# Start of a two-layer hybrid encoder: halves of x in two transfers each, squares on two engines, pair sums, constant products in the first norm, a weight split ahead of its root

## The chip, the cores and the metric

The kernel runs on one core of a Trainium2 chip. The metric is the device time of one execution in microseconds; less is better. TensorE (PE) multiplies, VectorE (DVE) and ScalarE (ACT) work elementwise, GpSimd (POOL) helps, SyncE (SP) issues most of the loads. All data are float32.

## What is computed

Two encoder layers over 512 positions of 1024 channels. The part that matters here is the start of the first layer: the norm of x, the product with the input projection `w_in`, and, for the memory branch, the norm of the memory tokens.

```python
def rms_norm(x, g):
    xf = x.astype(jnp.float32)
    y = xf * lax.rsqrt(jnp.mean(xf * xf, axis=-1, keepdims=True) + RMS_EPS)
    return (y * g.astype(jnp.float32)).astype(x.dtype)

mem_n = rms_norm(mem, mem_norm_g)
for l in range(DEPTH):
    h = rms_norm(x, g_pre_mix[l])
    proj = h @ w_in[l]
    q_a, k_a, v_a, q_b, k_b, v_b, q_m, gate_pre = jnp.split(proj, splits, axis=-1)
    ...                       # three attention branches (the third into mem_n), gates, output projection
    x = x + rms_norm(merged @ w_out[l], g_post_mix[l])
    ...                       # gated MLP with a depthwise convolution
    x = x + rms_norm(f @ w_down[l], g_post_ffn[l])
```

## The kernel before

x lies transposed, channels on the partitions: eight blocks of 128 channels (k = 0 to 7) by 512 positions, in two halves of 256 positions (`HALVES`). Every product is made three times: a weight and an activation are each split into a high part (a cast to the faster matmul type, on ScalarE) and a low part (the difference to it, on VectorE or GpSimd), and `mm3` adds high by high, high by low and low by high. `split` does the cast and the difference; `weights` loads a weight of 128 x 1024 (three buffers `wraw`) and splits it, for the first group in two pieces of 512 columns each (tiles `m`).

The start of the program, in the order of its code: `load_x` issues the first half of x from SyncE in four transfers of two blocks; two constant products (`idle`) run on TensorE; `first_squares` squares the eight blocks on ScalarE and adds neighbours in pairs on VectorE; `pre_norm_job` makes the norm. Its `rstd_job` sums over the channels by products with a constant column (`mean`; these are the sums spoken of later), takes the root on ScalarE and the reciprocal on VectorE, and spreads the result over the partitions by two transposes on TensorE. Then, for each k, VectorE multiplies x with the gain and this row (`normed`), ScalarE casts it to the high part of h, VectorE makes the low part.

The first six output tiles of `w_in` (`FIRST`) are made by `run_group`, in three pairs, first for the first half of the positions and then for the second: 8 blocks x 2 tiles x 3 products = 48 products for each pair and half. For the second half the squares stand behind the first half's last cast of h; their sums are two times two products.

What the order is decided by: each engine runs its instructions in the order of the program. `Woven` holds jobs (generators) with a due time on a clock that counts TensorE's planned cost; `tick` and `need` run the jobs whose time has come and so place their instructions in the order. The second half's `pre_norm_job` is spawned with a delay of `SD1`, the norm of the memory tokens (`mem_norm_job`: four loads issued by ScalarE, eight squares, seven adds, the sums) with 6.0. `Counted` books the planned time of ScalarE and VectorE for the due times of other jobs. A scheduler below orders instructions of one engine by their dependences and the order of the code. `wraw` has three buffers, so the load of the fourth weight waits for the differences of the first.

Of the kernel before, what the change touches and what calls it, by code (L numbers as in the profile page):

```python
# [9 lines left out]
AF = mybir.ActivationFunctionType  # L10
# [10 lines left out]
KD = D_MODEL // 128  # L21
# [4 lines left out]
HALVES = (slice(0, 256), slice(256, 512))  # L26
FULL = slice(0, 512)
FIRST = (0, 3, 4, 7, 6, 1)
# [3 lines left out]
V_PRE, V_POST, V_PREF, V_POSTF, V_BG, V_CW, V_CB = 0, 8, 16, 24, 32, 56, 188  # L32
# [3 lines left out]
LAT_QK, LAT_SM, LAT_T, LAT_V, LAT_T2 = 1.0, 4.5, 1.5, 2.0, 0.6  # L36
STEP_A, STEP_B, STEP_M = 9.0, 9.0, 5.5
SQG, LOG, GEN, KVE = {0: (), 1: ()}, {0: (), 1: ()}, 'GGVGVG', 'VVGG'
SD1 = 4.0
MARGIN = 0.3  # L40
SB = True
TAILG = (0, 2, 4, 6)
# [77 lines left out]
def tile_hybrid_encoder(ctx, tc, xT, memT, memg, vecs, rpb, w_in, w_kv, w_bra, w_brb, w_brm,  # L120
                        w_out, w_up, w_down, c_ident, c_mask, c_tab0, c_tab1, out):
    nc = tc.nc
# [14 lines left out]
    wv = Woven(tc)  # L137

    def nm(s):
        uid[0] += 1  # L140
        return f"{s}_{uid[0]}"
# [11 lines left out]
    def ytile(shape=(128, 512)):  # L153
        return tp.tile(list(shape), F32, tag="y", name=nm("y"), bufs=8)
# [4 lines left out]
    def smalls(n=2):  # L159
        return sp.tile([128, n], F32, tag="st", name=nm("st"))  # L160
# [7 lines left out]
    def tbank(shape=(128, 512)):  # L168
        return ps_t.tile(list(shape), F32, tag="pt", name=nm("pt"))

    def obank(p=64):
        return ps_o.tile([p, 512], F32, tag="o", name=nm("o"))
# [5 lines left out]
    ACT, V = Counted(nc.scalar, wv, 0.1, 0.8e-3), Counted(nc.vector, wv, 0.065, 1.05e-3)  # L178
# [8 lines left out]
    xs = const.tile([128, 2, KD, 256], F32, name="x")  # L187

    def xh(k, half):
        return xs[:, half.start // 256, k, :]  # L190

    def load_x(half):
        for k in range(0, KD, 2):
            i = half.start // 256
            nc.sync.dma_start(out=xs[:, i, k:k + 2, :], in_=xT[:, i, k:k + 2, :])

    g0 = const.tile([128, KD], F32, name="g0")
    nc.scalar.dma_start(out=g0, in_=vecs[:, 0, V_PRE:V_PRE + KD])
    load_x(HALVES[0])
    eps = const.tile([128, 1], F32, name="eps")  # L200
    nc.gpsimd.memset(eps, RMS_EPS)
# [25 lines left out]
    def weights(src, K, C, slot=None, eng=None, after=None):  # L227

        raw = wp.tile([128, K, C], F32, tag="wraw", name=nm("wraw"))
        nc.sync.dma_start(out=raw, in_=src)  # L230
        if slot is None:
            hi = wp.tile([128, K, C], F32R, tag="whi", name=nm("whi"), bufs=2)
            lo = wp.tile([128, K, C], F32R, tag="wlo", name=nm("wlo"), bufs=2)
            split(raw, hi, lo, eng)
            behind(last_copy[0], after)
            return [(hi[:, k, :], lo[:, k, :]) for k in range(K)]
        n = 512 // C
        w = []
        for k in range(0, K, n):
            c = min(n, K - k)  # L240
            hi, lo = slot(F32R, (128, c, C)), slot(F32R, (128, c, C))
            split(raw[:, k:k + c, :], hi, lo, eng)
            w += [(hi[:, i, :], lo[:, i, :]) for i in range(c)]
        return w

    def mm(ps, a, b, first, last, cost):
        wv.pe(nc.tensor.matmul(ps, a, b, start=first, stop=last), cost)  # L247
# [75 lines left out]
    def acctile():  # L323
        return small("acc", 2, (128, 512))

    def rstd_job(accs, n, box):

        nb = n // 128
        bank = tbank((128, n + nb))
        pr, pt = bank[:, 0:n], bank[:, n:n + nb]  # L330
        for i, a in enumerate(accs):
            for b in range(nb):
                mm(pt[:, b:b + 1], a[:, 128 * b:128 * b + 128], mean, i == 0 and b == 0,
                   i == len(accs) - 1 and b == nb - 1, 0.11)
        rs = smalls(nb)
        crit[0] = ACT.activation(rs, pt, AF.Sqrt, bias=eps, scale=1.0).ins
        V.reciprocal(rs, rs)
        yield 0.8
        for b in range(nb):
            one = rs[:, b:b + 1]  # L340
            spread = bass.AP(one.tensor, one.offset, [list(one.ap[0]), [0, 128]])
            wv.pe(nc.tensor.transpose(pr[:, 128 * b:128 * b + 128], spread, ident), 0.11)
        box.append(pr)

    def normed(src, g, rs, hi, lo, eng=None):
        h32 = small("h32", 3)
        V.scalar_tensor_tensor(out=h32, in0=src, scalar=g, in1=rs, op0=ALU.mult, op1=ALU.mult)
        split(h32, hi, lo, eng)
# [7 lines left out]
    def rtile():  # L356
        return tp.tile([128, 512], F32, tag="R", name=nm("R"), bufs=1)
# [3 lines left out]
        V.tensor_mul(y, ps, R)  # L361
        return y

    def pre_norm_job(l, goff, acc, hs, i):
        half, box = HALVES[i], []
        yield from rstd_job(acc if isinstance(acc, list) else [acc[:, half]], 256, box)
        for k in range(KD):
            g = g0[:, k:k + 1] if l == 0 and goff == V_PRE else vec[:, l, goff + k:goff + k + 1]
            normed(xh(k, half), g, box[0], hs[k][0][:, half], hs[k][1][:, half],
                   G if k in LOG[l > 0 and goff == V_PRE] else V)  # L370
        crit[0] = last_copy[0]
        yield 1.2
        wv.give(f"h{l}.{goff}.{i}")
# [5 lines left out]
    def end_job(l, goff, og, acc, acc2, i, then, lat, more=()):  # L379
        half, box = HALVES[i], []  # L380
        yield lat
        yield from rstd_job([acc[:, half]] + list(more), 256, box)
        for k in range(KD):
            V.tensor_mul(og[k][:, half], og[k][:, half], box[0])
            (G if then is None and i and k in TAILG else V).tensor_add(xh(k, half), xh(k, half), og[k][:, half])
            if acc2 is not None:
                sumsq_add(acc2[:, half], xh(k, half), k == 0, None, G if k in SQG[goff == V_POSTF] else V)
            else:
                nc.sync.dma_start(out=out[:, k, half], in_=xh(k, half))
        if then is not None:  # L390
            yield 9.0
            yield from then(i)

    def factor_end_job(l, goff, og, acc, acc2, i, nxt):

        half, box = HALVES[i], []
        gnext, h, R = nxt
        yield ready(1.4)
        yield from rstd_job([acc[:, half]], 256, box)
        for k in range(KD):  # L400
            V.tensor_mul(og[k][:, half], og[k][:, half], box[0])
            V.tensor_add(xh(k, half), xh(k, half), og[k][:, half])
            raw_split(l, gnext, k, xh(k, half), h[k][0][:, half], h[k][1][:, half])
            if k == 0:
                yield 0.6
            wv.give(f"h{l}.{gnext}.{i}.{k}")
            yield 1.05
        for k in range(KD):
            sumsq_add(acc2[:, half], xh(k, half), k == 0)
        yield 3.5  # L410
        box = []
        yield from rstd_job([acc2[:, half]], 256, box)
        ACT.copy(R[:, half], box[0])
        if i == 1:
            yield 0.6
            wv.give(f"R{l}.{gnext}")
# [30 lines left out]
    def h_tiles():  # L447
        return [(htile(), htile()) for _ in range(KD)]
# [46 lines left out]
    def group_weights(srcs, engs):  # L495
        return [weights(s, KD, 128, big, e) for s, e in zip(srcs, engs)]
# [368 lines left out]
    def first_squares(half):  # L865
        sqs = [ytile((128, 256)) for _ in range(KD)]
        for k in range(KD):
            ACT.activation(sqs[k], xh(k, half), AF.Square)
            if k % 2:
                V.tensor_add(sqs[k], sqs[k], sqs[k - 1])  # L870
            if k in (3, 5) and half != HALVES[0]:
                V.tensor_add(sqs[k], sqs[k], sqs[k - 2])
        return sqs[1::2] if half == HALVES[0] else sqs[5::2]

    idle_bank = obank(128)

    def idle(n):

        one, none = mean[:, 0:1], zero[:, 0:1]
        a, b = (bass.AP(t.tensor, t.offset, [list(t.ap[0]), [0, w]]) for t, w in ((one, 128), (none, 512)))  # L880
        for _ in range(n):
            mm(idle_bank, a, b, True, True, 0.0)

    idle(2)
    hs = h_tiles()
    wv.spawn(pre_norm_job(0, V_PRE, first_squares(HALVES[0]), hs, 0))
    gw = group_weights([w_in[0, m] for m in FIRST[:2]], (V, V))
    load_x(HALVES[1])
    nc.sync.dma_start(out=vec, in_=vecs)
    nc.gpsimd.tensor_scalar_mul(hb, vec[:, :, V_BG:V_CW], 0.5)  # L890
    wv.need(f"h0.{V_PRE}.0")
    with tc.issue_after(last_copy[0]):
        sqs = first_squares(HALVES[1])
    wv.spawn(pre_norm_job(0, V_PRE, sqs, hs, 1), SD1)
    gw += group_weights([w_in[0, m] for m in FIRST[2:]], (V, G, V, G))
# [6 lines left out]
    for l in range(depth):  # L902
# [29 lines left out]
        acc = [None] * KD  # L932
# [20 lines left out]
        hs, R, gw = h_tiles(), rtile(), []  # L953
# [17 lines left out]
        for j in range(NFF):  # L971
            pair = []
            for m in (j, j + NFF):
# [3 lines left out]
                w = ahead.pop()  # L977
# [24 lines left out]
        else:  # L1002
            hm, km, vm = [], [], []
            wv.spawn(mem_norm_job(l + 1, hm, htile), 20.0)
            pre, R, raw, box = [], rtile(), [], []
# [5 lines left out]
            gw = []  # L1011
# [19 lines left out]
            hs = box  # L1031
# [93 lines left out]
```

## Time and profile before

| | |
|---|---|
| median of 3 runs | 1551.7 us (1549.61, 1551.70 and 2167.76) |
| profiled execution, its own time | 1551.73 us |
| its span | 1550.0 us |
| TensorE busy | 1522.5 us, 98% |
| VectorE busy | 951.6 us, 61% |
| ScalarE busy | 712.7 us, 46% |
| GpSimd busy | 149.7 us, 10% |
| share of TensorE in the chain that ended last | 91% |

The chain is followed back from the last instruction, at each step to what released it. Times in the rows are microseconds from the start of the span. A product of float32 columns that isn't in the faster type shows as two records, so two sums show as x4.

### The profile page before, as it was taken

The page shows a single profiled execution, that of the slowest core. Times are in us where ns is not written, and L with a number is a line of the kernel's source. Part 1 is how long each engine was busy: PE and PEld are TensorE (multiplying, and loading weights), DVE is VectorE, ACT ScalarE, POOL GpSimd, SP SyncE. Part 2 cuts the span into 40 slices and gives each one's busy share as a digit, 9 for nine tenths or more (in the row PEclk, how much of TensorE's full clock was granted, in tenths as well). Part 3 has the DMA queues.
Part 4 walks back from the last instruction along what each step waited for, and adds up shares of the span by engine and source line. Part 5 has one row for each costly group of instructions (what it writes and reads, how often), then busy time and mean ns, then how long its engine had stood idle before and what let it go on. Part 6 is the DMA issues. An engine that isn't in the chain of part 4 may idle for free.

```text
span 1550.0 us, 20648 instructions
## 1 busy us (share of the span) xinstructions
PE 1522.5 (98%) x7970; PEld 1300.1 (84%) x7970; DVE 951.6 (61%) x1684; ACT 712.7 (46%) x1266; POOL 149.7 (10%) x217
## 2 busy tenths in 40 slices
PE   8999999999999999999989999999999999999997
PEld 7988888888988888888888888888889888888887
DVE  6685676335777777742497756753456977776233
ACT  5565554336544444532355555532354544444231
POOL 3340000110000000000154300002100000000000
PEclk9999999999999999999999999999999999999999
DMA  7221213235113322333431221132350233323331
GB/s 246 89 88 64 62 57 107 84 95 165 53 59 100 100 96 95 118 90 101 129 102 59 78 66 58 61 104 88 102 177 15 82 96 99 101 99 89 99 105 63
DMA packets 45810, 144.91 MB, mean 93 GB/s; under 512 B 5376, under 2 KB 9600, under 8 KB 45712
## 3 DMA queue, kind: packets, MB, share of 16 engines
q1 hardware_dynamic: 43776, 139.85, 28.5%
q10 hardware_dynamic: 1296, 2.10, 0.4%
q0 software_dynamic: 640, 1.64, 0.3%
q8 instruction: 62, 1.02, 0.3%
q14 instruction: 36, 0.29, 0.1%
HBM read 141.48 MB, written 2.10 MB: 93 GB/s over the span
## 4 chain that ended last, share of the span: by engine, by line
PE 91%; DVE 6%; ACT 2%; issue 1%; DMA 0%; SPq 0%; ACTq 0%; DVEq 0%
PE mm L247 80%; PE s L247 4%; PE o L247 3%; PE pt L258 2%; DVE m L114 1%; DVE y L114 1%; PE pt L247 1%; DVE ka L114 1%; DVE x L114 1%; ACT y L114 1%; DVE st L114 0%; DVE acc L114 0%; DMA x<-in_xT_dram 0%; DVE wlo L114 0%; ACT whi L114 0%
## 5 line engine op out<-in xcount | busy, mean ns | idle before, releaser
L247 PE MATMUL mm<-h,whi 128*128 128x512 f32 x2496 | 776.5, 392 | 0.0
L247 PEld LDWEIGHTS mm<-h,whi 128*128 128x128 f32 x2496 | 462.0, 188 | 91.3
L247 PE MATMUL mm<-h,wlo 128*128 128x512 f32 x1248 | 486.9, 390 | 0.0
L114 DVE TENSOR_TENSOR wlo<-wraw,whi 128x1024 fp32r<-128x1024 f32 (+1 forms) x213 | 259.2, 1217 | 284.7 <-ACT whi L114 282.3
L114 ACT CAST whi<-wraw 128x1024 fp32r<-128x1024 f32 (+1 forms) x213 | 221.4, 1040 | 307.8 <-PE mm L247 293.4
L247 PEld LDWEIGHTS mm<-h,wlo 128*128 128x128 f32 x1248 | 234.5, 188 | 49.6
L247 PE MATMUL mm<-m,whi 128*128 128x512 f32 (+1 forms) x800 | 215.1, 356 | 1.0 <-DVE m L114 0.8
L247 PEld LDWEIGHTS mm<-m,whi 128*128 128x128 f32 x800 | 141.8, 189 | 22.8 <-PE mm L247 1.3
L247 PE MATMUL mm<-m,wlo 128*128 128x512 f32 (+1 forms) x400 | 142.1, 355 | 0.0
L114 DVE SCALAR_TENSOR_TENSOR y<-y,vec,y 128x511 f32<-128x511 f32 x176 | 130.5, 748 | 3.5 <-ACT y L114 0.9
L114 DVE TENSOR_TENSOR y<-mm,R 128x512 f32<-128x512 f32 x82 | 56.4, 688 | 68.5 <-PE mm L247 68.5
L247 PEld LDWEIGHTS mm<-m,wlo 128*128 128x128 f32 x400 | 75.5, 189 | 10.9
L802 POOL TENSOR_TENSOR m<-m,y 128x512 f32<-128x512 f32 x28 | 36.1, 1289 | 399.4 <-DVE y L114 399.4
L114 ACT ACTIVATE y<-y,vec 128x512 f32<-128x512 f32 x88 | 71.1, 815 | 2.3 <-DVE y L114 1.9
L247 PE MATMUL mm<-m,m 128*128 128x512 f32 x240 | 63.5, 394 | 0.0
L114 ACT ACTIVATE y<-y 128x512 f32<-128x512 f32 x44 | 27.9, 633 | 71.7 <-DVE y L114 71.3
L114 ACT CAST m<-pt 128x512 fp32r<-128x512 f32 (+1 forms) x72 | 38.6, 541 | 46.8 <-PE pt L258 38.5
L114 ACT ACTIVATE y<-y,st 128x256 f32<-128x256 f32 (+1 forms) x80 | 43.8, 549 | 30.4 <-DVE st L114 28.9
L114 DVE TENSOR_TENSOR acc<-acc,sq 128x256 f32<-128x256 f32 (+1 forms) x80 | 41.1, 514 | 26.6 <-ACT sq L114 24.7
L114 DVE TENSOR_TENSOR m<-pt,m 128x512 fp32r<-128x512 f32 (+1 forms) x72 | 45.1, 630 | 19.9 <-ACT m L114 18.6
L114 ACT CAST m<-y 128x512 fp32r<-128x512 f32 x32 | 19.9, 622 | 72.5 <-DVE y L114 72.5
L247 PE MATMUL mm<-h,m 128*128 128x256 f32 x312 | 49.1, 301 | 2.0 <-ACT h L114 1.0
(154 smaller groups left out, 1789.9 us busy)
## 6 DMA issues: line engine op xcount, KB each, us to landing
wraw<-in_w_in_dram SPq DMA_DIRECT2D x88, 512.0 KB, 3.7
wraw<-in_w_up_dram SPq DMA_DIRECT2D x88, 512.0 KB, 3.6
wraw<-in_w_down_dram SPq DMA_DIRECT2D x32, 512.0 KB, 3.5
wraw<-in_w_out_dram SPq DMA_DIRECT2D x16, 512.0 KB, 3.9
wraw<-in_w_down_dram SPq DMA_DIRECT2D x16, 384.0 KB, 3.1
wraw<-in_w_kv_dram SPq DMA_DIRECT2D x8, 512.0 KB, 4.0
wraw<-in_w_bra_dram SPq DMA_DIRECT2D x16, 192.0 KB, 2.3
x<-in_xT_dram SPq DMA_DIRECT2D x8, 256.0 KB, 7.3
```

What stands on the lines that cost most here:

```text
L114: return op(*args, **kw)
L247: wv.pe(nc.tensor.matmul(ps, a, b, start=first, stop=last), cost)
L258: wv.pe(nc.tensor.transpose(ps[:, 128 * i:128 * i + 128], s, ident), 0.11)
L802: (V if br == 2 and m >= 6 else G).tensor_add(acc[m], acc[m], gs)
```

## The change

`load_x` brings each half of x in two transfers of four blocks. In the first half, `first_squares` squares blocks 3 and 7 on VectorE instead of ScalarE; the pair sums stay. `rstd_job` can be given `idle` as `warm` and then puts constant products of 256 columns between its own: one after the second pair sum, one after the reciprocal, two after the transposes; only the first norm does so. The first weight's split is written ahead of the first norm's job, the second behind it. `SD1` is 5.0 instead of 4.0.

```diff
-SD1 = 4.0
+SD1 = 5.0
...
     def load_x(half):
-        for k in range(0, KD, 2):
+        for k in range(0, KD, 4):
             i = half.start // 256
-            nc.sync.dma_start(out=xs[:, i, k:k + 2, :], in_=xT[:, i, k:k + 2, :])
+            nc.sync.dma_start(out=xs[:, i, k:k + 4, :], in_=xT[:, i, k:k + 4, :])
...
-    def rstd_job(accs, n, box):
+    def rstd_job(accs, n, box, warm=None):
...
+            if warm and i == 1:
+                warm(1, 256)
         rs = smalls(nb)
         crit[0] = ACT.activation(rs, pt, AF.Sqrt, bias=eps, scale=1.0).ins
         V.reciprocal(rs, rs)
+        if warm:
+            warm(1, 256)
         yield 0.8
...
+        if warm:
+            warm(2, 256)
         box.append(pr)
...
         for k in range(KD):
-            ACT.activation(sqs[k], xh(k, half), AF.Square)
+            if half == HALVES[0] and k in (3, 7):
+                V.tensor_mul(sqs[k], xh(k, half), xh(k, half))
+            else:
+                ACT.activation(sqs[k], xh(k, half), AF.Square)
...
-    def idle(n):
+    def idle(n, w=512):
...
-            mm(idle_bank, a, b, True, True, 0.0)
+            mm(idle_bank[:, 0:w], a, b, True, True, 0.0)
...
-    wv.spawn(pre_norm_job(0, V_PRE, first_squares(HALVES[0]), hs, 0))
-    gw = group_weights([w_in[0, m] for m in FIRST[:2]], (V, V))
+    sqs = first_squares(HALVES[0])
+    gw = group_weights([w_in[0, FIRST[0]]], (V,))
+    wv.spawn(pre_norm_job(0, V_PRE, sqs, hs, 0, idle))
+    gw += group_weights([w_in[0, FIRST[1]]], (V,))
```

What this does to the order is seen at three places. The first is ScalarE around the root of the first half's norm (`st` from `pt`); `y` are the squares, `wraw_148` and `wraw_158` the first and the second weight, `m` their high parts, `h_112` and `h_114` the first high parts of h. Before:

```order
L114 ACTIVATE y_134<-x 128x256
L114 ACTIVATE y_135<-x 128x256
L114 ACTIVATE st_183<-pt_174,eps 128x2
L114 CAST m_150<-wraw_148 128x512
L114 CAST m_154<-wraw_148 128x512
L114 CAST h_112<-h_39_188 128x256
L114 CAST m_160<-wraw_158 128x512
L114 CAST h_114<-h_40_192 128x256
```

Of the change (the first weight is now `wraw_146`, the second `wraw_156`):

```order
L114 ACTIVATE y_131<-x 128x256
L114 ACTIVATE y_132<-x 128x256
L114 CAST m_148<-wraw_146 128x512
L114 ACTIVATE st_180<-pt_170,eps 128x2
L114 CAST m_152<-wraw_146 128x512
L114 CAST m_158<-wraw_156 128x512
L114 CAST m_162<-wraw_156 128x512
L114 CAST h_110<-h_39_188 128x256
```

The cast of half the first weight has moved ahead of the root, and all four casts of the two weights now stand ahead of the first cast of h.

The second place is TensorE at the end of the first pair of tiles (`mm_285` and `mm_286`) for the first half, where the sums of the second half's squares stand (`pt` from `mean` and `y`). Before:

```order
L247 MATMUL mm_286<-h_124,m_165 128x256
L247 MATMUL pt_333<-mean,y_225 128x1 x2
L247 MATMUL pt_333<-mean,y_227 128x1 x2
L247 MATMUL mm_285<-h_126,m_154 128x256
L247 MATMUL mm_285<-h_127,m_154 128x256
```

Of the change:

```order
L247 MATMUL mm_286<-h_124,m_163 128x256
L247 MATMUL pt_339<-mean,y_225 128x1 x2
L247 MATMUL pt_339<-mean,y_227 128x1 x2
L247 MATMUL o_287<-h_110,m_244 128x256
L247 MATMUL o_287<-h_111,m_244 128x256
```

Before, `h_124` is block 6 of h and the six products of block 7 (`h_126`, `h_127`) follow the sums; in the change `h_124` is block 7, so all 48 products of the pair stand ahead of the sums and the next pair's follow.

The third place is ScalarE after that, at the second half's norm. `h_112`, `h_114` and so on are again the high parts of h, now of the second half; `m_387` to `m_393` are the memory tokens, `h_95_395` and `sq` their squares, `wraw_272` the sixth weight of the group. Before:

```order
L114 CAST h_112<-h_83_355 128x256
L114 CAST h_114<-h_84_359 128x256
L114 CAST m_274<-wraw_272 128x512
L114 CAST m_278<-wraw_272 128x512
L114 CAST h_116<-h_85_363 128x256
L455 DMA m_387<-in_memT_dram 128x512
L114 CAST h_118<-h_86_367 128x256
L114 CAST h_120<-h_87_371 128x256
L455 DMA m_389<-in_memT_dram 128x512
```

Of the change, from the last of the four loads on (`m_359`; `whi` are the first two weights of the memory branch):

```order
L461 DMA m_359<-in_memT_dram 128x512
L114 ACTIVATE h_87_361<-m_353 128x256
L114 ACTIVATE sq_88_363<-m_353 128x256
...
L114 ACTIVATE sq_93_378<-m_359 128x256
L114 CAST h_110<-h_95_392 128x256
L114 ACTIVATE sq_94_381<-m_359 128x256
L114 CAST h_112<-h_96_396 128x256
L114 CAST whi_702<-wraw_700 128x1024
L114 CAST whi_743<-wraw_741 128x1024
L114 CAST h_114<-h_97_400 128x256
```

The casts of the second half's h have moved behind the memory loads and seven of the eight squares of the memory tokens, and from the third on behind two whole weight casts too; VectorE's differences and adds stand in the same new order.

## Rows read from the trace of the kernel before

**Rows 1.** The page: busy time of each engine, chain by engine.

```profile
PE 1522.5 (98%) x7970; PEld 1300.1 (84%) x7970; DVE 951.6 (61%) x1684; ACT 712.7 (46%) x1266; POOL 149.7 (10%) x217
PE 91%; DVE 6%; ACT 2%; issue 1%; DMA 0%; SPq 0%; ACTq 0%; DVEq 0%
```

**Rows 2.** The chain in order of time, 0 to 100 us: start, length, what.

```profile
2.12 6.74 DMA x<-in_xT_dram
...
23.54 1.05 PE pt L247 x8
...
37.15 5.04 PE mm L247 x42
42.19 0.34 PE pt L247 x4
```

**Rows 3.** Transfers by issue window: the first weight; the first load of x's second half.

```profile
wraw<-in_w_in_dram SPq DMA_DIRECT2D x1, 512.0 KB, 7.5
...
x<-in_xT_dram SPq DMA_DIRECT2D x1, 256.0 KB, 8.6
```

**Rows 4.** Timeline, 0 to 30 us: start, length, engine, line, what, idle before.

```profile
0.74 1.81 SPq L195 DMA_DIRECT2D x<-in_xT_dram  x4
...
2.60 0.91 SPq L230 DMA_DIRECT2D wraw<-in_w_in_dram  x2
...
5.88 0.72 ACT L114 ACTIVATE y<-x 128x256 f32<-128x256 f32 x2 [0.47 <-DMA x<-in_xT_dram]
...
11.17 0.26 ACT L114 ACTIVATE st<-pt,eps 128x2 f32<-128x2 f32 x1 [1.56 <-PE pt L247]
...
11.68 0.69 PE L342 MATMUL pt<-ident,st 128*128 128x128 f32 x2 [0.56 <-DVE st L114]
12.41 0.48 DVE L114 SCALAR_TENSOR_TENSOR h<-x,g,pt 128x256 f32<-128x256 f32 x1 [0.78 <-PE pt L342]
...
14.87 7.81 PE L247 MATMUL mm<-h,m 128*128 128x256 f32 x41 [0.91 <-DVE h L114]
...
20.44 2.57 ACT L114 ACTIVATE y<-x 128x256 f32<-128x256 f32 x8
...
21.28 2.54 DVE L114 TENSOR_TENSOR y<-y,y 128x256 f32<-128x256 f32 x6
```

**Rows 5.** Constant products; then busy time of tile mm by stretch, granted clock.

```profile
0.95 3.78 PE L247 MATMUL o<-zero,mean 128*128 128x512 f32 x4 [0.95 <-POOL zero L206]
...
14.87:17.62 2.75, 2.75 (x12) 2.69 (x12) 0.00 (x0) 0.00 (x0) 1.00 0.64 206
...
20.00:22.68 2.68, 2.68 (x22) 2.48 (x20) 0.00 (x0) 0.00 (x0) 1.00 0.88 337
```

**Rows 6.** VectorE's groups, 12 to 24 us: count, busy us, mean ns, idle before.

```profile
L114 DVE TENSOR_TENSOR m<-wraw,m 128x512 fp32r<-128x512 f32 x6 | 4.1, 689 | 0.0
L114 DVE SCALAR_TENSOR_TENSOR h<-x,g,pt 128x256 f32<-128x256 f32 x8 | 3.6, 471 | 0.8 <-PE pt L342 0.8
L114 DVE TENSOR_TENSOR h<-h,h 128x256 fp32r<-128x256 f32 x8 | 3.2, 414 | 0.0
```

**Rows 7.** Timeline, 29 to 42 us, of the second half's norm and the memory tokens.

```profile
29.57 0.33 ACTq L455 DMA_DIRECT2D m<-in_memT_dram  x1
...
32.85 0.80 ACT L114 CAST h<-h 128x256 fp32r<-128x256 f32 x2 [1.25 <-DVE h L114]
33.13 1.08 DVE L114 TENSOR_TENSOR h<-h,h 128x256 fp32r<-128x256 f32 x3
...
41.38 2.35 DVE L114 TENSOR_TENSOR wlo<-wraw,whi 128x1024 fp32r<-128x1024 f32 x2
```

**Rows 8.** Transfers by issue window: memory loads (one, three), one late weight.

```profile
m<-in_memT_dram ACTq DMA_DIRECT2D x1, 256.0 KB, 5.2
m<-in_memT_dram ACTq DMA_DIRECT2D x3, 256.0 KB, 5.9
...
wraw<-in_w_in_dram SPq DMA_DIRECT2D x1, 512.0 KB, 3.6
```

More of the change, by code (lines that the diff above doesn't have):

```diff
@@ L362, in scaled, with pre_norm_job @@
         return y
-    def pre_norm_job(l, goff, acc, hs, i):
+    def pre_norm_job(l, goff, acc, hs, i, warm=None):
         half, box = HALVES[i], []
-        yield from rstd_job(acc if isinstance(acc, list) else [acc[:, half]], 256, box)
+        yield from rstd_job(acc if isinstance(acc, list) else [acc[:, half]], 256, box, warm)
         for k in range(KD):
@@ L875, in tile_hybrid_encoder @@
     idle_bank = obank(128)
-    def idle(n):
+    def idle(n, w=512):
         one, none = mean[:, 0:1], zero[:, 0:1]
-        a, b = (bass.AP(t.tensor, t.offset, [list(t.ap[0]), [0, w]]) for t, w in ((one, 128), (none, 512)))
+        a, b = (bass.AP(t.tensor, t.offset, [list(t.ap[0]), [0, w]]) for t, w in ((one, 128), (none, w)))
         for _ in range(n):
-            mm(idle_bank, a, b, True, True, 0.0)
+            mm(idle_bank[:, 0:w], a, b, True, True, 0.0)
     idle(2)
     hs = h_tiles()
-    wv.spawn(pre_norm_job(0, V_PRE, first_squares(HALVES[0]), hs, 0))
-    gw = group_weights([w_in[0, m] for m in FIRST[:2]], (V, V))
+    sqs = first_squares(HALVES[0])
+    gw = group_weights([w_in[0, FIRST[0]]], (V,))
+    wv.spawn(pre_norm_job(0, V_PRE, sqs, hs, 0, idle))
+    gw += group_weights([w_in[0, FIRST[1]]], (V,))
     load_x(HALVES[1])
```

## Prediction

> **What bounds the kernel now.** I read the page's busy shares and chain first, then the chain in order of time, then the timeline of the first 45 us, and last the landings of single transfers. TensorE is busy for 1522.5 us, 98% of the span, and carries 91% of the chain that ended last [rows 1]. So the reader is to see that little is left outside TensorE, and that the change, whose code all lies ahead of the first 45 us, can at most move the point from which TensorE runs without a break. The chain shows that point. It runs through the fourth transfer of x until 8.86, through squares, sums and the first norm, and meets TensorE for good at 23.54, where the sums of the second half's squares begin [rows 2]. From there TensorE never waits until 42.19, when 42 of the 48 products of the second half's first pair of output tiles are done [rows 2]. After that the order of every engine is the same as before, so I compare the two kernels at that event: each microsecond there is one in the end. The sum is made against the profiled execution's 1551.73 us; the median of the three runs is 1551.70, so no correction is needed.
>
> **First half, up to its root.** Today the last 256 KB of the first half of x land 6.7 us after their issue at 2.12 [rows 2], though the third transfer had landed by 5.88 [rows 4]. Now the same last bytes are in the second of two transfers. Its issue comes at about 1.18 instead of 2.12, since four issues took 1.81 us, 0.47 each [rows 4], and two go. The bounds are 5.88 (the landing of the third piece) and 8.86 (that of the fourth). The nearest row is the fourth's own 6.74 us, as the bytes and their place behind the others are the same, so I take 1.18 + 6.74 = 7.92.
>
> From landing t, the old chain needs two squares, an add, two sums, root (at 11.17), reciprocal and two transposes (to 12.37): t + 2.3 at the root, t + 3.5 at the end [rows 4]. Now three squares stand on ScalarE (k = 4, 5, 6; one more at 0.32, which is 2.57 / 8) while VectorE squares k = 7 beside them; so t + 2.6 = 10.5 at the root and t + 3.8 = 11.7 at the end. The square moved to VectorE thus saves one of four, but four pieces arrive at once where two did. The constant product after the reciprocal is half as wide as one of the two that took 3.78 us [rows 5], so 0.95 us at that pace; it can hold the transposes by 0.2 us, which VectorE hides: it is still in the second weight difference until 11.9. The two later constant products end at 13.8, before the first low part of h (14.4, below). Without those covers they would cost up to 0.2 and 1.9 us.
>
> **The weight split ahead of the root.** ScalarE now casts half of the first weight before the root, so the root waits for that weight if it is late. The first weight took 7.5 us from 2.60 [rows 3, 4]; issued 0.94 earlier it lands at 9.2, the cast's 0.52 of issue room ends at 9.7, and the root is due at 10.5. So it holds nothing, with 0.8 us to spare. VectorE does the difference in its idle time. But on ScalarE three more weight casts now stand ahead of the first cast of h, so the first low part of h comes at 14.4; today TensorE has it at 14.87 [rows 4]. (The chain: root 10.5, casts 0.52 apart, the last of the three ends at 12.3, the cast of h behind it at 12.8; VectorE from 11.9 on has two norm products, two weight differences and this low part, 2.7 us by their means [rows 6], 2.4 with the overlap shown below.)
>
> **From there to the sums of the second half.** VectorE worked from 12.41 to 21.37 without idle time on 8 products with the norm, 8 low parts and 5 weight differences, 9.0 us for 10.2 us of busy time (3.6, 3.2 and five sixths of 4.1 [rows 6]), as they overlap. After the root it still has 8, 8 and 5 (the first has gone ahead, but the difference m_249 has come in), of which one (m_153) runs in the 0.7 us of the transposes. So it starts its norm products at 11.9, needs 8.3 us and ends at 20.2, 1.2 us earlier. ScalarE is free for the second half's squares some 1.2 us before that, at 19.0, and finishes them by 21.6. The six adds (2.54 us [rows 4]) then end at 22.7 on VectorE, which now is the later of the two; today they end at 23.82. TensorE's four sums end 0.77 later, at 23.5 against 24.59 [rows 2]. With SD1 at 5.0 all 48 products of the first pair stand before these sums, where 42 did. The 6 that no longer follow are 0.72 us at 0.12 each [rows 2]. Today 102 products and two transposes lie between 24.59 and the second half's first product at 37.15 [rows 2], 12.56 us; now 6 products fewer, so the second half can begin at 23.5 + 11.84 = 35.3. This part gains 1.8 us.
>
> **What the moved spawn does to the second half.** The larger SD1 also puts the memory norm's start ahead of the second half's norm. ScalarE then has, in this order: four loads of the memory tokens, seven squares of them, and only then the first cast of h for the second half; two whole weight casts stand before the third. Today those casts ended at 33.65, 3.5 us before TensorE wanted the first of them, and the memory squares came after [rows 7]. The new chain: sums at 23.5; root, then casts at 0.52 each, so the last weight cast starts at 25.3; four issues of 0.33 behind it, the last at 26.3. Its landing is bounded by 5.2 us (the first such load) and 8.6 (the longest of an x transfer, in the crowd at the start); I take 5.9, the median of the other three [rows 3, 8], so 32.2. The seventh square and the cast follow, and VectorE starts the first low part at 33.0. Up to its last low part it then has 8 low parts of 0.36, 3 adds and 6 norm products of 0.42, and 2 whole weight differences of 1.18 [rows 4, 7]: 2.9 + 1.3 + 2.5 + 2.4 = 9.0 us. The last low part ends at 42.0 and the seventh of eight at 41.6; after the seventh the five products that need it or follow it take 0.6 us, so the 42 products are done at 42.2. Unhindered they would be done at 35.3 + 5.04 = 40.3, so TensorE waits 1.9 us in pieces, mostly before the low parts k = 2 and k = 4, each behind a weight difference. Who waits behind these waits: ScalarE's casts of the two kv weights, whose products stand behind all pairs of the second half, so nobody.
>
> **The sum.** At the event of 42.19 the new kernel stands at 42.2: 1.8 us gained by a first half that ends earlier and hands 6 products less to the time behind its sums, and 1.9 us given back because h of the second half comes late. That is +0.0 against 1551.73, so **1551.7 us**. The other edits cost nothing: the first constant product lies where TensorE waits for the second transfer anyway (from about 6 to 8 us), and the two issues saved in the second half of x hand over data that is not squared before 19.0.
>
> **The rivals.** First, *x lands early*: the second transfer comes at 5.88, as its bytes arrive in one run. Everything up to the event moves by 2.04, to 1549.7. For it: the third piece was there 4.2 us after its issue at about 1.65 [rows 4]. Against it: the fourth took 6.74.
> Second, *the second half does not wait*: the memory loads land within 4.0 us, as a lone weight did in 3.6 [rows 8], and the casts of h are in time: 1551.7 - 1.9 = 1549.8. Against it: the four share the DMA engines with two kv weights.
> Third, *slower: the memory loads crowd*. They land 8.6 us after issue, as the first load of the second half of x did [rows 3]. The price is 8.6 - 5.9 = 2.7 us, so 1554.4; from a landing of 5.9 us on the event comes later than today. For it: four loads and two weights, 2 MB, now leave within a few microseconds, where today the four were spread from 29.57 on, one after another behind casts [rows 7]. Beside it stands a sentence of the Trainium skill, "DMA: Bandwidth & Descriptors", section "Issuing engines are not separate DMA queues": loads issued by ScalarE interleave with those of SyncE on the same DMA engines, so a queue of their own does not shield them. No run here shows yet by how much.
> Fourth, *TensorE's pace*. In 14.87 to 17.62 it issued 12 products in 2.75 us, from 20.00 on 22 in 2.68; the granted clock reads 1.00, the 2.4 GHz level, in both [rows 5], so the count tells more here than the column. If the first pair kept the slow 0.23 us to its end, its 48 would end at 14.4 + 11.0 = 25.4 and hold the sums by 2.7 us: 1554.4. If the pace rises at 20 as today, they end at 22.9 and cost 0.2; if the constant products raise it earlier, nothing is gained, as the sums wait for 22.7 anyway. The Trainium skill's "TensorE: Matmul & The Clock Gate", section "Part 1: The HAM clock gate", says that an idle array runs at half clock and that sustained work releases it; by that rule short constant products with pauses between them buy little, and the trace agrees in so far as the two wide ones at the start left the pace slow at 14.87.
> Fifth, *x lands as late as it did*: 8.86, since larger transfers need not end sooner. Then 0.94 of the gain is missing: 1552.6.
>
> **How the numbers follow.** Forecast 0.38, early x 0.20, no wait 0.17, crowded loads 0.10, slow pace 0.05, late x 0.10. By its own costs the forecast goes from 1551.0 (memory loads at 5.2) to 1552.6 (x at 8.86). The range takes in both cases just below 1550 and, beside an early x, loads at 5.2 (another 0.7 lower) and 0.4 of the 2.1 us between the two close runs shown: 1548.6. Above, it takes in the crowded loads and the slow pace: 1554.5. A change of 2%, about what a measurement of this kernel can tell from no change, would be 31 us, and no case comes near: faster 0.01, same 0.98, slower 0.01.
>
> **What would show it.** Right: the four sums of the second half start near 22.7; the last load of memory tokens lands near 32; TensorE's first products of the second half start near 35.3 and show gaps behind low parts of h. Wrong: the second transfer of x well off 7.9; the root waiting for the first weight; no gaps between 35 and 42; or the event of 42.19 moved by more than 1 us, which would make the second half's delay, the step that I hold for the least sure, the wrong one.

## The result, and the profile after

The changed kernel takes 1555.26 us (median of 22 runs, 1550.34 to 1560.37), the kernel before 1551.36 in the same comparison. The ratio is 1.0026, with a 95% interval of 1.0019 to 1.0034: 3.9 us slower. 1551.7 was predicted, with a range up to 1554.5. The runs of the change lie 10 us apart; those of before, one at 2167.76 left aside, 4.7; in the later comparisons those of before lie 4.8 to 8.8 us apart.

I have two profiles of the changed kernel: one of an execution with a span of 1551.2 us, and one taken later (below) with 1553.8, which lies nearer to the median. The page of the first, its busy shares and its chain, against [rows 1]:

```profile
PE 1525.0 (98%) x7978; PEld 1302.2 (84%) x7978; DVE 952.8 (61%) x1686; ACT 710.2 (46%) x1264; POOL 150.5 (10%) x217
PE 91%; DVE 6%; issue 1%; ACT 1%; DMA 1%; POOL 0%; ACTq 0%; DVEq 0%; POOLq 0%
```

Little here tells the two kernels apart. TensorE is busy for 2.5 us more, and the four new constant products, eight records, alone took 0.68 + 1.20 + 1.74 = 3.6. The chain in order of time (start, length, what) shows the difference, against [rows 2]:

```profile
6.70 0.54 PE o L247 x2
...
8.30 1.06 PE o L247 x2
...
19.64 1.84 DVE y L114 x2
21.53 1.02 PE pt L247 x4
...
24.53 6.84 DMA m<-in_memT_dram
...
43.80 0.34 PE pt L247 x4
```

In [rows 2] the chain comes to TensorE at 23.54 and stays there. Now it leaves TensorE again for the last load of the memory tokens and the second half's h, and TensorE takes it over only at the end of the first pair. The event by which I compared the kernels, 42 products of that pair done, is at 43.80 instead of 42.19. The timeline (start, length, engine, line, what, idle before), against [rows 4, 7]:

```profile
5.68 1.03 ACT L114 ACTIVATE y<-x 128x256 f32<-128x256 f32 x3 [0.25 <-DMA x<-in_xT_dram]
...
7.35 0.62 ACT L114 CAST m<-wraw 128x512 fp32r<-128x512 f32 x1 [0.64 <-DMA wraw<-in_w_in_dram]
...
8.34 0.26 ACT L114 ACTIVATE st<-pt,eps 128x2 f32<-128x2 f32 x1 [0.37 <-PE pt L247]
...
20.12 0.61 PE L247 MATMUL pt<-mean,y 128*128 128x1 f32 x4 [1.06 <-DVE y L114]
21.53 1.01 PE L247 MATMUL pt<-mean,y 128*128 128x1 f32 x4 [0.80 <-DVE y L114]
...
30.95 5.92 PE L247 MATMUL s<-h,m 128*128 128x256 f32 x48
36.71 3.16 PE L247 MATMUL mm<-h,m 128*128 128x256 f32 x25
...
40.77 3.02 PE L247 MATMUL mm<-h,m 128*128 128x256 f32 x17 [0.90 <-DVE h L114]
```

x came early: the second transfer was there at 5.7. The first weight at 7.3 did not hold the root, which waited for TensorE. The second half then starts at 36.9 and stops for h. (The timeline lets a product start up to 0.16 us before the one ahead of it ends; I count from that end, 30.95 + 5.92 = 36.87, as the chain in [rows 2] does.) Its 42 products take 43.80 - 36.87 = 6.9 us instead of 5.04 [rows 2]. The granted clock is the other new thing. Columns: stretch, its length, PE busy (instructions), granted clock, DMA share, GB/s.

```profile
20.00:22.00 2.00, 1.08 (x7) 0.81 0.54 207
22.00:24.00 2.00, 2.00 (x10) 0.50 0.32 50
...
26.00:28.00 2.00, 2.00 (x11) 0.50 0.98 293
28.00:30.00 2.00, 2.00 (x19) 0.98 1.02 366
```

Each of TensorE's two groups of sums stands behind a pause, of 1.06 and 0.80 us, and the clock fell to the 1.2 GHz level for some 6 us: 10 and 11 products in 2 us, 19 at the 2.4 GHz level. From the end of the sums at 22.55 to 36.87 lie 14.3 us for what takes 11.84 at full pace, so 2.5 us were lost there.

### The profile page after: what moved, and what is told of

It is laid out like the page before. It is cut to its first block, busy times and chain, and to the rows that moved or that the text cites. A ratio compares the mean times of both kernels' runs of the same rounds, so it can differ in the third digit from the quotient of the medians.

```text
span 1551.2 us, 20650 instructions
## 1 busy us (share of the span) xinstructions
PE 1525.0 (98%) x7978; PEld 1302.2 (84%) x7978; DVE 952.8 (61%) x1686; ACT 710.2 (46%) x1264; POOL 150.5 (10%) x217
## 4 chain that ended last, share of the span: by engine, by line
PE 91%; DVE 6%; issue 1%; ACT 1%; DMA 1%; POOL 0%; ACTq 0%; DVEq 0%; POOLq 0%
PE mm L247 80%; PE s L247 4%; PE o L247 3%; PE pt L258 2%; DVE y L114 1%; DVE m L114 1%; PE pt L247 1%; DVE h L114 1%; DVE ka L114 1%; DVE x L114 1%; DVE acc L114 1%; DVE wlo L114 0%; DMA m<-in_memT_dram 0%; ACT whi L114 0%; ACT y L114 0%
## 5 line engine op out<-in xcount | busy, mean ns | idle before, releaser
L114 DVE TENSOR_TENSOR m<-wraw,m 128x512 fp32r<-128x512 f32 (+1 forms) x58 | 37.9, 668 | 24.0 <-ACT m L114 23.8
```

Source lines behind the costliest of these rows:

```text
L114: return op(*args, **kw)
```

## Experiments

Two theories stood against each other first. **A**: the second half's h is late, because SD1 at 5.0 puts it behind the memory tokens on ScalarE and VectorE. **B**: the clock that falls around the second half's sums costs the time. All comparisons are with runs of the kernel before on the same chip.

**SD1 alone, on the kernel before.**

```diff
-SD1 = 4.0
+SD1 = 5.0
```

> The kernel before with SD1 5.0 and nothing else. Theory A: the second half's casts of h come behind the memory squares as in the change; by the chain of the prediction the sums end at 24.6, the last load of the memory tokens lands 8.7 later, the 42 products are done 18.7 after the sums: 43.3 against 42.19, so about 1552.5, and the spread of the runs widens as the change's did. Rival C: SD1 alone is harmless or gains the 0.7 us of six products: 1550.7 to 1551.4, spread as before.

Measured: 1557.35 us, ratio 1.0043 (1.0030 to 1.0057), 6.7 us slower. The chain of this kernel:

```profile
27.12 9.23 DMA m<-in_memT_dram
...
42.52 2.96 DMA wraw<-in_w_kv_dram
45.47 0.94 DVE h L114
...
48.94 0.34 PE pt L247 x4
```

The last of the four loads takes 9.2 us here, where I had 5.9. The chain then names a load of a kv weight, which would have held VectorE until 45.5. The timeline does not bear that out: VectorE worked without a pause from 38.47 to 47.5, and ScalarE had cast both kv weights of that stretch before 41.

```profile
38.47 0.76 DVE L114 TENSOR_TENSOR h<-h,h 128x256 fp32r<-128x256 f32 x1 [0.79 <-ACT h L114]
...
41.45 4.67 POOL L599 TENSOR_TENSOR y<-mask,y 128x256 f32<-128x256 f32 x3 [2.00 <-DVE h L114]
...
43.86 1.68 DVE L114 TENSOR_TENSOR wlo<-wraw,whi 128x1024 fp32r<-128x1024 f32 x1
45.46 1.28 DVE L114 TENSOR_TENSOR h<-h,h 128x256 fp32r<-128x256 f32 x2
```

The event, expected at 43.3, is at 48.94. The last load landed 3 us later than expected, the first low part stands 2.1 us behind it instead of 0.8, and VectorE's chain of low parts took 10.0 us instead of 9.0, slow beside GpSimd. The one number is enough to make the kernel slower than the whole change does.

**SD1 undone, in the change.**

```diff
-SD1 = 5.0
+SD1 = 4.0
```

> The change with SD1 back at 4.0, all else kept: the sums of the second half stand again behind 42 products, and the memory norm behind the second half's norm. Theory A (the longer time comes from the second half's norm, which SD1 at 5.0 puts behind the memory loads and squares): the loss goes, 1551 to 1552, near the kernel before, and between 33 and 43 us TensorE shows no gap behind h. Rival (one of the other parts costs the time: large transfers, the constant products, the squares on VectorE, or the first weight's cast ahead of the root): it stays at 1554 to 1556. If the other parts are a gain of their own, as my sum had it (0.7 to 2 us), 1549.5 to 1551.

Measured: 1551.45 us, ratio 1.0001 (0.9990 to 1.0012). The whole loss is SD1's, and at this SD1 the other parts together are worth nothing that can be measured. In its profile TensorE runs through the pair:

```profile
35.17 5.04 PE mm L247 x42
```

This execution, the fastest of the ten, has a span of 1545.6 and its event at 40.21, 2.0 us ahead of [rows 2]; its clock did not fall behind the sums. (Its span is 4.4 us shorter; the rest is far behind the event, see the last section.) The runs of this kernel go from 1547.5 to 1553.8, so what the other parts gain is had in some of them at most.

**The memory norm later, SD1 left at 5.0.**

```diff
-    wv.spawn(mem_norm_job(0, hm, big), 6.0)
+    wv.spawn(mem_norm_job(0, hm, big), 8.0)
```

> The change with the memory norm spawned at 8.0 instead of 6.0: the 48 products stay ahead of the sums, but the second half's casts of h stand ahead of the memory squares again. Theory A (the late second-half norm costs): the wait of TensorE at 37 to 44 us (7.09 us for 42 products that need 5.04 in the change's trace) goes, 42 products done near 41.8 instead of 43.80, so 2.0 us below the change, near 1553.2, and the spread of the runs narrows. Theory B (only the clock that fell to 0.50 from 21.6 to 28.0 costs): the norm in time gains nothing that lasts, time stays near 1555. Rival C (the larger transfers of x scatter the time): near 1555, spread as wide as the change's 10 us.

Measured: 1551.48 us, ratio 1.0001 (0.9992 to 1.0011). Its chain passes the second half's first pair without a break:

```profile
37.23 5.76 PE mm L247 x48
```

So A holds: what costs is not that 48 products stand ahead of the sums, but that the memory norm stands ahead of the second half's.

**Constant products around the second half's sums.**

```diff
+            if keep:
+                idle(keep[i], 256, keep_bank)
...
-    wv.spawn(pre_norm_job(0, V_PRE, sqs, hs, 1), SD1)
+    wv.spawn(pre_norm_job(0, V_PRE, sqs, hs, 1, None, (2, 2)), SD1)
```

Two of 256 columns stand ahead of each of the two sums, in a bank of their own.

> The change with constant products of 256 columns in a bank of their own, two ahead of each of the two sums of the second half, so that TensorE does not idle from 18.9 to 21.5. The granted clock should then read 1.00 where the change had 0.50 (21.6 to 28.0), and the second half's products can begin near 34.2 instead of 36.7. Theory A: the event of 43.80 is set by memory loads, squares and casts and stays within 0.5 us, so time near 1555. Theory B: the 2.5 us that the slow products cost come off, 1552.8.

Measured: 1558.12 us, ratio 1.0040 (1.0026 to 1.0055). The clock stays at 1.00 from 20 to 36 us, and it is not faster:

```profile
26.15 8.35 DMA m<-in_memT_dram
...
44.45 4.00 PE mm L247 x17
```

TensorE reaches the second half earlier, and waits longer for an h that isn't there; then the clock falls in these pauses, and 17 products take 4.00 us instead of 2.04. The event did not stay within 0.5 us of 43.80, as A expected; it is at 48.45, since the last load landed at 34.5, 3.1 us later than in the first profile of the change, and the last products were slow. B alone is wrong: as long as h sets the event, TensorE's pace ahead of it is worth nothing.

**Both.** The two edits above together.

> The change with both edits: memory norm at 8.0 and constant products at the sums. If A and B hide each other, this gains both: second half from 34.2, 42 products done at 39.3 against 42.19 of the kernel before, so 2.9 us below it, near 1548.5. If only A counts, as with the later memory norm alone (1553.2); if only B counts, 1552.8; rival C: near 1555 with the spread of the change.

Measured: 1549.45 us, ratio 0.9993 (0.9983 to 1.0003), in the medians 2.0 under the later memory norm alone. The two intervals overlap, so that the clock counts once h is in time is likely by the times, and not shown. The chains say it for one execution each: from the end of the sums, at 23.35, to the second half's first product lie 11.85 us, with the later memory norm alone 13.34.

```profile
35.20 5.76 PE mm L247 x48
```

**Memory loads issued early.** ScalarE issues the four loads right behind the second half's squares; the jobs stay in the change's order. `mem_loads` holds the loop that was at the head of `mem_norm_job`.

```diff
     with tc.issue_after(last_copy[0]):
         sqs = first_squares(HALVES[1])
+        raws = mem_loads(big)
```

> The change with the four loads of the memory tokens issued by ScalarE right behind the second half's squares, some 4 us earlier, ahead of the root; the order with SD1 at 5.0 stays, memory squares and two kv casts ahead of most of h. If the landing of these loads is what makes h late (theory A in its narrow form), the last lands before 28, the casts of h end near 31 and the low parts near 40, the stall goes or falls under 0.5 us, and the time to 1550.5 to 1552. If it is the length of the work queued ahead of h on VectorE and ScalarE that makes it late, gaps behind h stay between 36 and 43 and the time stays above 1553.5. In both cases the granted clock still falls behind the sums, some 2.5 us.

Measured: 1553.08 us, ratio 1.0019 (1.0009 to 1.0028). The chain:

```profile
22.11 0.52 ACT m L114
...
22.70 1.29 POOL m L225
...
24.03 0.58 PE pt L247
...
37.33 5.04 PE mm L247 x42
```

The stall behind h is gone, 5.04 us for 42, as A in its narrow form says. The time did not fall as far as expected, because the scheduler, with the loads in front, moved the third weight's casts behind the squares: TensorE now waits 1.22 us for that cast and 0.57 for GpSimd's difference, at 22.7 and 24.0. The order is nearly the change's, but its ten runs lie only 3.4 us apart, where the 22 of the change lie 10. With the same constant products around the sums in addition:

> The run before with four constant products around the second half's sums in addition, as in the earlier run that had them alone. If h is in time now, the clock that stays at 1.00 behind the sums is worth what it was worth beside the later memory norm, 2 us: 1548.5 to 1550. If h is still late, TensorE reaches h's gaps earlier and the gain goes into them: as the run without, within 0.7 us.

Measured: 1552.74 us, ratio 1.0021 (1.0011 to 1.0030). No gain: the new wait stands behind the constant products, and the clock fell there.

**Without the constant products of the first norm,** beside the later memory norm.

```diff
-    wv.spawn(pre_norm_job(0, V_PRE, sqs, hs, 0, idle))
+    wv.spawn(pre_norm_job(0, V_PRE, sqs, hs, 0))
```

> The change with the memory norm at 8.0, as run earlier (1551.48), and without the four constant products of the first norm. If these raise TensorE's pace in the first pair, the first pair is slower without them and the sums may come up to 2 us later: 1552 to 1553.5. If they only hold the transposes (0.5 us here) and the pace rises by itself, 1551 or a little less.

Measured: 1548.74 us, ratio 0.9991 (0.9978 to 1.0004), in the medians 2.7 under the same with them. The same edit at SD1 = 4.0:

> The change with SD1 at 4.0 and without the constant products of the first norm. If the constant products cost time by themselves, by holding the transposes and so h of the first half, this is 1548.5 to 1550 beside 1551.45 with them. If what they cost came from their place beside a norm that is moved, or from the spread of single runs, it stays at 1551 to 1552.

Measured: 1550.16 us, ratio 0.9993 (0.9984 to 1.0002), in the medians 1.3 under the same with them, which ran on another chip. Both point the same way, but the intervals overlap those of the kernels with them, and neither leaves out no change. The constant products are not seen to pay; that they cost time is likely and not shown. What two of them can cost is seen in the second profile below.

**The best of it**: memory norm at 8.0, constant products around the second half's sums, none in the first norm.

> The change with the memory norm at 8.0 and the four constant products of 256 columns around the second half's sums, and without the four of the first norm: the two edits that helped, together. If they add (the sums' products keep the granted clock, worth 2.0 us beside the later memory norm; the first norm's, left out, worth 2.7), 1546.5 to 1548, faster than the kernel before by 2 to 4 us. If both work by the same thing (the gap ahead of the sums, in which the clock falls or not), no more than one of them is had: 1548.5 to 1549.5.

Measured: 1549.05 us, ratio 0.9988 (0.9979 to 0.9997): 1.9 us faster than the kernel before. It is the one version of those tried whose whole interval lies below 1, and by little. The two edits do not add to more than either had. The chain of this kernel joins TensorE at 13.23 and stays:

```profile
13.23 8.09 PE mm L247 x51
...
34.92 5.76 PE mm L247 x48
```

**x in two transfers alone,** on the kernel before.

```diff
-        for k in range(0, KD, 2):
+        for k in range(0, KD, 4):
...
-            nc.sync.dma_start(out=xs[:, i, k:k + 2, :], in_=xT[:, i, k:k + 2, :])
+            nc.sync.dma_start(out=xs[:, i, k:k + 4, :], in_=xT[:, i, k:k + 4, :])
```

> The kernel before with x in two transfers for each half and nothing else. If the second transfer lands near 5.7, as it did in the changed kernel, instead of 8.9, and the first half's chain carries that through to the sums, up to 2 us are gained: 1549 to 1550. If the first weight, or the granted clock behind the sums, takes the gain, no change: 1551 to 1552.

Measured: 1551.08 us, ratio 0.9992 (0.9983 to 1.0002). The chain and the clock:

```profile
22.92 1.14 PE mm L247 x6
...
36.98 5.04 PE mm L247 x42
```

```profile
24.00:26.00 2.00, 2.00 (x12) 0.50 0.79 227
```

The sums end at 22.92 instead of 24.59 [rows 2], 1.7 us earlier. But TensorE now pauses for 1.22 and 0.80 us ahead of their two groups, and the clock falls: the 102 products to the second half take 14.06 us, not 12.56. Of 1.7 us gained 1.5 are gone in this execution, and the event is at 42.02 against 42.19.

**The changed kernel again,** for a second profile.

> The changed kernel itself, for a second profile, since its runs spread over 10 us (1550.3 to 1560.4) and the profile at hand is of a mild one (span 1551.2, last memory load landed at 31.4, 42 products done at 43.8). If the landing of the memory loads and what it delays makes the spread, the span moves with the event of the 42 products, one for one, and this event with the landing of the last memory load within 1 us: a span of 1556 would show a landing near 34 to 36 and gaps of 5 us or more behind h. If the spread comes from TensorE's clock elsewhere or from the rest of the program, the span moves and the event does not.

Its span is 1553.8 us, its time 1555.58. The chain:

```profile
7.47 1.06 PE o L247 x2
8.53 1.50 PE pt L247 x8
10.03 1.06 PE o L247 x2
...
26.08 7.94 DMA m<-in_memT_dram
...
43.97 2.49 PE mm L247 x17
46.46 0.34 PE pt L247 x4
```

The last load lands at 34.02, 2.65 later than in the first profile; the event, at 46.46, is 2.66 later, and the span 2.6. Here 2.6 us of the spread are followed to their root, in two executions. The last load is issued 1.55 later, as the first norm's sums and constant products ran at half the pace (the sums took 1.87 and 1.50 us instead of 1.05 and 1.06, the constant product between them 1.06 instead of 0.54, the one behind them 1.06 in both, and the root came at 10.06, not 8.34), and it took 1.10 us longer. TensorE waited 4.2 us for h, not the 5 or more that were expected of a slow execution.

## Why the prediction was wrong

The steps, as forecast and in the two profiles (us):

| | forecast | first | second |
|---|---|---|---|
| second transfer of x landed | 7.9 | 5.7 | 5.6 |
| first weight landed | 9.2 | 7.3 | 7.2 |
| root of the first half | 10.5 | 8.3 | 10.1 |
| sums of the second half end | 23.5 | 22.5 | 23.9 |
| last load of memory tokens issued | 26.3 | 24.5 | 26.1 |
| the same landed | 32.2 | 31.4 | 34.0 |
| first low part of the second half starts | 33.0 | 32.2 | 34.9 |
| last low part ends | 42.0 | 43.3 | 45.9 |
| second half's first product | 35.3 | 36.9 | 37.2 |
| 42 products done | 42.2 | 43.8 | 46.5 |

**The step that failed** is "What the moved spawn does to the second half". Its mechanism was right, and it was the step that I held for the least sure; two terms of its sum were too small. The 9.0 us of VectorE from the first to the last low part were 11.1 in both profiles. And the loads were landed at 32.2 by a price of 5.9 us; 6.8 and 7.9 were measured in the change, 8.4 and 9.2 in two experiments. In the first profile the last load was issued 1.8 us earlier than forecast and so landed early all the same; there the longer chain alone made the event late. With the landing (-0.8 in the first, +1.8 in the second), the chain (+2.1) and the last products behind it (+0.3) the event comes out at 43.8 and 46.4, as measured. The stall put down at 1.9 us was 1.9 and 4.2; in the first profile it was no longer only because TensorE itself, slowed by its clock, came to the second half at 36.9 and not at 35.3.

**Why the chain was longer.** I priced its low parts at 0.36 us from a stretch in which GpSimd stood still [rows 7]. In the second profile nearly all of the extra is theirs; in the first they have half of it, and weight differences and adds the rest, all beside GpSimd. The timeline of the second profile:

```profile
34.57 2.50 POOL L605 TENSOR_TENSOR y<-mask,y 128x256 f32<-128x256 f32 x3 [5.63 <-issue]
...
34.85 0.73 DVE L114 TENSOR_TENSOR h<-h,h 128x256 fp32r<-128x256 f32 x1 [1.60 <-ACT h L114]
...
36.39 0.95 DVE L114 TENSOR_TENSOR h<-h,h 128x256 fp32r<-128x256 f32 x1
...
39.51 2.75 POOL L605 TENSOR_TENSOR y<-mask,y 128x256 f32<-128x256 f32 x3 [1.95 <-DMA y<-in_rpb_dram]
39.86 1.81 DVE L114 TENSOR_TENSOR h<-h,h 128x256 fp32r<-128x256 f32 x2
41.59 0.86 DVE L114 SCALAR_TENSOR_TENSOR h<-x,g,pt 128x256 f32<-128x256 f32 x2
...
43.51 0.75 DVE L114 TENSOR_TENSOR h<-h,h 128x256 fp32r<-128x256 f32 x2
44.18 0.86 DVE L114 SCALAR_TENSOR_TENSOR h<-x,g,pt 128x256 f32<-128x256 f32 x2
45.12 0.82 DVE L114 TENSOR_TENSOR h<-h,h 128x256 fp32r<-128x256 f32 x2
```

Two low parts take 1.81 us beside GpSimd and 0.75 when it is idle. The products with the norm, which read one of their two blocks from PSUM, TensorE's result memory (`pt`), take 0.86 for two in both places. The transfers do not explain it: the DMA engines were busier beside the last pair of low parts (share 0.69 from 44 to 46, 0.82 us for the two) than beside the slow pair (0.54 from 40 to 42). In the kernel before, the second half's low parts were done at 34.2 [rows 7], and GpSimd began on these masks at 38.85:

```profile
38.85 2.32 POOL L599 TENSOR_TENSOR y<-mask,y 128x256 f32<-128x256 f32 x3 [6.48 <-DVE h L114]
```

The change brought the two together. The Trainium skill, "SBUF — State Buffer", section "Who interferes with whom", says that a VectorE instruction with two inputs in SBUF contends with a GpSimd instruction that reads SBUF. The trace agrees, by a factor of 2.4 here. No run here took GpSimd's work away, so that it is the cause is read from these prices, and not shown by an experiment.

**Step by step.** The early x, a rival at 0.20, came true (5.7 where I said 5.88), but it did not give its 2.0 us: the sums ended at 22.5 and 23.9, near the forecast 23.5. What ate it differs. In the second profile it is the first norm: its sums ran at half pace, and two constant products lay on the chain with 1.06 us each, where I had costed them at nothing ("where TensorE waits for the second transfer anyway", "VectorE hides" the 0.2 us); the root came 4.5 us after the landing, where I had 2.6. In the first profile the root came nearly on time, 2.7 us after the landing; the constant product behind it held the transposes by 0.3 us. In both, the six adds took 3.42 us instead of 2.54 [rows 4], beside GpSimd's differences. That the first weight holds nothing was right in both profiles of the change; in three experiments (both edits, memory loads issued early, and SD1 = 4.0 without constant products) it landed at 8.0, 7.8 and 7.6 and lay on the chain. That the forecast of these sums was nearly met is two errors that cancel.

**The rivals.** "The memory loads crowd", at 0.10 and 8.6 us of landing, is the one that came nearest: both its place and its sign are right, and its sum, 1554.4, lacks the longer chain on VectorE. I priced the loads from executions in which they left one after another; issued within 1.9 us, beside kv weights, they cost what the longest rows showed. "TensorE's pace stays slow" was looked for in the first pair; the clock's fall behind the sums, 2.5 us, was in no rival. Had h been in time, TensorE would have come to the second half that much earlier; behind a late h, what it costs goes into the wait. "The second half does not wait" was excluded by every profile with the change's order.

**The range** was too narrow, because it took single rivals at its ends. The late landing and the longer chain come together: both follow from moving h behind the memory norm.

## What to carry to other kernels

When a change moves a chain of work to another time, price each instruction by the engines that will run beside it there, and a load by the others in flight, not by the means of the place it leaves. Look first at what now sets the event: the same constant products shortened TensorE's way to the second half by 1.5 us, and with h late the event did not come earlier for it. And an earlier arrival upstream of a fixed later one becomes a pause; on TensorE a pause can cost the clock, and with it the gain.

## What the runs showed of the hardware that I had not expected

The granted clock of TensorE fell to 0.50 behind the second half's sums in both profiles of the change and in seven of the experiments, for some 3 to 7 us, and in four it did not. The length of the pauses alone does not tell which: it was kept behind pauses of 0.55 and 0.81 us (SD1 undone) and fell behind 0.35 and 0.80 (later memory norm, no constant products in the first norm). In the three profiles in which constant products filled these pauses and no other wait came behind them, it stayed at 1.00. The Trainium skill's "TensorE: Matmul & The Clock Gate", section "Part 1: The HAM clock gate", has an idle array at half clock; these traces agree in the direction, but do not give a pause that decides. What else decides it stays open.

The prediction took the event for the whole of the difference ("each microsecond there is one in the end"); by the profiles this holds only within some 2 us. The granted clock also falls near 875 us, far behind the changed code, in nine of the fourteen profiles, those of the kernel before and of the change among them, and not in the other five. Before, and with SD1 undone:

```profile
870.00:880.00 10.00, 7.91 (x40) 0.83 0.21 73
870.00:880.00 10.00, 9.45 (x55) 1.00 0.23 66
```

Between the event and the end of the span lie 1507.1 to 1509.7 us in the nine and 1505.3 to 1506.7 in the five. So the shortest spans, 1545.5 to 1546.6 (both edits, SD1 undone, the best), owe a part to a clock that falls or stays far behind the edits, and the price of an edit is better read from the event than from the span of a single profile. Which part of the change's spread of 10 us is the clock's and which the loads' stays open; in the two profiles of it the event followed the landing of the last memory load one for one.
